# Routing one half of the heads per copy of a sample's rows, narrower projections, and S5's zeroth powers as copies, in a two-layer decoder step

## The chip, the cores and the metric

One core of a Trainium2 chip. The metric is the device time of one execution in microseconds (us), lower is better. Engines: PE (TensorE), DVE (VectorE), ACT (ScalarE), POOL (GpSimd) and SP (SyncE, which only issues DMAs). Each engine runs its own instructions in the order in which the program gives them.

## The reference

One inference step of a decoder with two layers. There are 512 prompt tokens and 64 sample tokens (8 sequences of 8), 576 in all, of width 1024.

- Layer 0 mixes tokens with S5, a grouped complex-diagonal state space (64 groups of 16 channels, 64 states each), then a GLU. Layer 1 mixes them with causal pooling over 2, 4, 8 or 16 tokens.
- After each mixer, and after each channel mixer, `x <- LN(ALPHA * x + f(x))`.
- The channel mixer of both layers is PEER: `q = x @ w_q` gives 8 heads of two halves of 128. Each of these 16 halves (chunks `c` below, head `c // 2`) is scored against 128 keys; the best 16 of each half are kept; of the 16 x 16 sums per head the best 16 are kept. These name 128 x 128 experts: `idx = i1 * 128 + i2`, `gate = softmax(best)`, `out = sum(gate * gelu(x . u[idx]) * v[idx])`.

```
s = einsum('thid,hind->thin', q, keys)
top_s, top_i = top_k(s, 16)
cand_s = top_s[:, :, 0, :, None] + top_s[:, :, 1, None, :]
best_s, best_j = top_k(cand_s, 16)
```

## The kernel before, in words

The tokens stand in five tiles of 128 rows. Tiles 0 to 3 are the prompt. Tile 4 holds the 64 sample tokens twice: rows 0 to 63 and rows 64 to 127 are copies. So 640 columns are projected (`NX`; `NT` is 576, `ND` is 384, the columns of tiles 0 to 2). Products are made from a high and a low part of each operand (`xH`, `xL` and `wh`, `wl`), three matmuls for one; `wl` is a subtraction on DVE, or on POOL for the weights `w_q`.

**S5.** `params` makes the powers 0 to 8 of the state matrix (`PW`). While PE projects the input, eight weights `m` of 128 columns in two halves each, `back(q)` makes on DVE the tile `BL` (powers 7 down to 0 times `bb`, four buffers, two a call) and `turn(q)` transposes it on PE into `BT`; ACT copies it out. `udone(m)` writes the projection to DRAM (`du`); it is read back as `U8`, half of the groups after `m = 3` and the other half after `m = 7`, eight DMAs each. Then `taps` makes `CL` on DVE (powers 0 to 8 times `c`), `inputs` multiplies `BT` with `U8` into `HS`, `toeplitz` makes `KT`, and `steps` runs the recurrence on DVE. The last `swap` (a DMA from `HS` to `H`) lets PE make the outputs.

**Norm and projection.** `out_proj` calls `norms`: tile by tile a residual, the norm (`layer_norm`: lines 791 to 801, small steps on one column between two large ones), the transposes of the tile on PE, and the split into `xH` and `xL`. After tiles 3 and 4 `early(0, ND)` projects the first two chunks of `w_q` for tiles 0 to 2; these wait in `self.pre`.

**Routing.** `peer` first stores tiles 0 to 2 to DRAM (`XD`) and adds `xH` and `xL` back into `xT` on POOL (line 1049). Then comes a loop over the 16 chunks: PE projects chunk `c` (`projected`) and scores chunk `c - 1` (`scores`: five matmuls, copied by ACT into one of three buffers `sc`), and DVE takes the best 16 of chunk `c - 2` (`tops`: `top16` on five tiles, five instructions for each: `MAX8`, `FIND_INDEX8`, `MATCH_REPLACE8`, `MAX8`, `FIND_INDEX8`). Between them a generator, `routing`, is pulled at most six times for each chunk. It runs `stage2` (the sums, their best 16, the experts' numbers and the gates) for four heads at a time and five tiles (heads 0 and 1, then 2 and 3, each on 10 rows of 128 x 256), so both calls end at chunk 12. After the loop `stage2` runs for tiles 3 and 4 with heads 4 to 7 (8 rows), then for tiles 0 and 1, then 2. With the experts of tiles 3 and 4 known, POOL begins to gather their rows.

**What stands beside the routing.** After the loop PE works on up to 44 of the 128 blocks of `u` (`raw` matmuls), stored with `spill`. How many, and between which instructions the generator is pulled, is decided by a count of costs when the program is written, not by time. Then follow the `hots` (one-hot products), and the long loop over 128 blocks of `u` and `v`, bound by PE.

Of the kernel before, what the change touches and what calls it, by code (L numbers as in the profile page):

```python
# [39 lines left out]
BT, GB, HC, PW = 1, 32, 2.0, (1,)  # L40
GE, S3, S4 = 0.98, 100, 4
VL = (43, 44, 45)
ORDER = [a for a in range(128) if (a + 1) * NPO // 128 > a * NPO // 128]
ORDER += [a for a in range(128) if a not in ORDER]
OFF = [0, 16, 24, 29, 33, 36, 38, 40] + list(range(42, 50))
# [81 lines left out]
class K:  # L127
# [142 lines left out]
    def s5(self):  # L270
# [55 lines left out]
        def powered(jobs, a, b):  # L326

            def args(e, w):
                n, k = e.stop - e.start, len(range(9)[w])
                sh = [128, n, k, 16]  # L330
                pw = [PW[:, w, r, e].rearrange("p s e -> p e s")[:, :, :, None].to_broadcast(sh) for r in range(2)]
                return pw, [t[:, e, None, :].to_broadcast(sh) for t in (a, b)]
            todo = [(o, t) + args(e, w) for o, t, e, w in jobs]
            for o, t, pw, ab in todo:
                V.tensor_tensor(o, pw[0], ab[0], op=OP.mult)
            for o, t, pw, ab in todo:
                V.tensor_tensor(t, pw[1], ab[1], op=OP.mult)
            for o, t, pw, ab in todo:
                V.tensor_tensor(o, o, t, op=OP.subtract)

        def params():
# [14 lines left out]
                next(ex, None)  # L356
            for _ in ex:
                pass
            V.memset(PW[:, 0, 0, :], 1.0)
            V.memset(PW[:, 0, 1, :], 0.0)  # L360
            V.tensor_tensor(PW[:, 1, 0, :], mag, cs, op=OP.mult)
            V.tensor_tensor(PW[:, 1, 1, :], mag, sn, op=OP.mult)
            tmp = p2.tile([128, 4, 8, 16], F32, name="BL", bufs=4).rearrange("p a b c -> p a (b c)")[:, :, :64]
            for b in (1, 2, 4):
                sh = [128, b, 64]
                cmul(V, PW[:, b + 1:2 * b + 1, 0, :], PW[:, b + 1:2 * b + 1, 1, :],
# [3 lines left out]
            im = slice(64, 128)  # L370
            A.activation(b2[im], b2[im], AF.Copy, scale=-1.0)
            A.activation(c1[im], c1[im], AF.Copy, scale=-1.0)

            for h in range(2):
                rows, e = slice(64 * h, 64 * h + 64), slice(32 * h, 32 * h + 32)
# [18 lines left out]

            for h in range(2):
                e = slice(32 * h, 32 * h + 32)
                BL = p2.tile([128, 4, 8, 16], F32, name="BL", bufs=4)
                t = BL.rearrange("p e s j -> p (e s) j")
                V.tensor_tensor(bb[:, e], bc(fr[:, e]), b1[:, e], op=OP.mult)
                V.tensor_tensor(t, bc(fi[:, e]), b2[:, e], op=OP.mult)  # L400
                V.tensor_tensor(b1[:, e], bc(fi[:, e]), b1[:, e], op=OP.mult)
                V.tensor_tensor(b2[:, e], bc(fr[:, e]), b2[:, e], op=OP.mult)
                V.tensor_tensor(bb[:, e], bb[:, e], t, op=OP.subtract)
                V.tensor_tensor(b2[:, e], b2[:, e], b1[:, e], op=OP.add)

        def back(q):

            BL, tb = ([p.tile([128, 4, n, 16], F32, name=k, bufs=m)[:, :, :8] for _ in range(2)] for p, k, n, m in ((p2, "BL", 8, 4), (pc, "tb", 9, 2)))
            e = [slice(8 * q + 4 * i, 8 * q + 4 * i + 4) for i in range(2)]
            powered([(BL[i], tb[i], e[i], slice(7, None, -1)) for i in range(2)], bb, b2)  # L410
            return BL

        def turn(q, BL):
# [7 lines left out]
        def taps(q):  # L421

            for e0 in (8 * q, 32 + 8 * q):
                es = [slice(e0 + i, e0 + i + 4) for i in (0, 4)]
                powered([(CL[:, e], pc.tile([128, 4, 9, 16], F32, name="tb", bufs=2), e, slice(0, 9)) for e in es], c1, c2)


        params()
# [9 lines left out]
        def udone(m, o):  # L438
            uT = p2.tile([128, NT], F32, name="uT", bufs=2)
            for q in range(2):  # L440
                A.activation(uT[:, 288 * q:288 * q + 288], o[q][:, :288], AF.Copy)
            A.dma_start(du[128 * m:128 * m + 128, :], uT)
            if m % 4 == 3:
                g = slice(8 * (m - 3), 8 * m + 8)
                for s in range(8):
                    (G if m > 3 and s % 2 else S).dma_start(U8[16 * s:16 * s + 16, g, :], duv[s][:, g, :])

        first = self.W.next_raws(2)
        o = [[self.ps(), self.ps()] for _ in range(2)]
# [361 lines left out]
    def projected(self):  # L811

        if self.pre:
            w, o, a, b = self.pre.pop(0)
            c, d = (b, NX) if a == 0 else (0, a)
            outs = [(self.ps()[:, :d - c], slice(c, d))]
            self.proj(outs, w, self.xH, self.xL)
            outs.insert(0 if a == 0 else 1, (o[:, :b - a], slice(a, b)))
        else:
            outs = [(self.ps()[:, :b - a], slice(a, b)) for a, b in ((0, ND), (ND, NX))]  # L820
            self.proj(outs, self.W.next(), self.xH, self.xL)
        return outs

    def finish(self, res, ln, p, then, transposed):
# [37 lines left out]
                    for _ in tr[4]:  # L862
                        pass
        if transposed:
            self.early(ND, NX)
            for tt in range(3):
                for _ in tr[tt]:
                    pass
# [163 lines left out]
    def peer(self, layer):  # L1032
# [10 lines left out]
        SD = self.dram.tile([128, 128, ND], F32, name=f"SD{layer}")  # L1043
        XD = self.dram.tile([128, 3, D], F32, name=f"XD{layer}")
        p2 = self.pool(rt, "pr2")

        S.dma_start(XD, self.x012)
        xT = self.per.tile([128, KD, ND], F32, name="x012")
        G.tensor_tensor(xT, self.xH.main.bitcast(F32), self.xL.main.bitcast(F32), op=OP.add)
        pr = self.pool(rk, "pr")  # L1050

        it = pr.tile([128, 128], I32, name="it")
# [1 line left out]
        self.iota2 = p2.tile([128, 128, 2], F16, name="iota2")  # L1054
        A.activation(self.iota2, it[:, :, None].to_broadcast([128, 128, 2]), AF.Copy)

        tops_ = [[pr.tile([128, 2, 5, 4, 16] if q < 2 else [128, 5, 8, 16], dt, name=f"{n}{q}") for q in (0, 2)]
                 for n, dt in (("tv", F32), ("ti", U32))]
        tv, ti = (lambda tt, c, t=t: t[0][:, c // 4, tt, c % 4] if c < 8 else t[1][:, tt, c - 8] for t in tops_)
        LG = ExitStack()  # L1060
# [22 lines left out]
        kload(0)  # L1083
        kload(1)

        def scores(c, q):
            o = [self.psB(), self.psB()]
            sc = pq.tile([128, 5, 128], F32, name="sc", bufs=3)
            for tt in range(5):
                d = o[tt // 4][:, 128 * (tt % 4):128 * (tt % 4) + 128]  # L1090
                self.mm(d, q[:, 128 * tt:128 * tt + 128], keys[c // 4][:, c % 4, :], True, True)
            A.activation(sc[:, :4].rearrange("p a b -> p (a b)"), o[0], AF.Copy)
            A.activation(sc[:, 4], o[1][:, :128], AF.Copy)
            return sc

        def tops(c, sc):
            self.top16([(sc[:, tt], tv(tt, c), ti(tt, c)) for tt in range(5)])

        prev = prev2 = None
        for c in range(16):  # L1100
            outs = self.projected()
            self.W.ahead()
            if layer == 0:
                next(self.pt, None)
            if prev:
                s_ = (c - 1, scores(c - 1, prev))
                if c % 4 == 0 and c < 12:
                    kload(c // 4 + 1)
            q = pq.tile([128, NX], F32, name="q", bufs=2)
            for o, cols in outs:  # L1110
                A.activation(q[:, cols], o, AF.Copy)
            if prev2:
                tops(*prev2)
                self.scored = c - 2
                for _ in range(PA):
                    if self.half or next(bg) == STEP:
                        break
            prev2 = s_ if prev else None
            prev = q
# [237 lines left out]
    def routing(self, tops, p, pr, p2, rk, gidx, ggate, GD, kept, begin, ending):  # L1357
# [7 lines left out]
        for g in range(2):  # L1365
            while self.scored < 4 * g + 3:
                yield STEP
            yield from self.stage2(tv[0][:, g], ti[0][:, g], p2, [t[:, :, 32 * g:32 * g + 32] for t in out])
        self.half = 1
        yield 0.0  # L1370
        unit = lambda ts: self.stage2(tv[1][:, ts], ti[1][:, ts], p2, [t[:, ts, 64:] for t in out])
        i1, i2, gate = out
        yield from unit(slice(3, 5))
        for u in range(2):
            f = p2.tile([128, 128], F32, name="idf")
            V.scalar_tensor_tensor(f, i1[:, 3 + u], 128.0, i2[:, 3 + u], op0=OP.mult, op1=OP.add)
            if u == 0:
                V.tensor_copy(gidx[:, :128], f)
                V.tensor_copy(ggate[:, :128], gate[:, 3])
            else:  # L1380
                for q in range(2):
                    rows = slice(64 * q, 64 * q + 64)
                    V.tensor_copy(gidx[rows, 128:], f[rows, rows])
                    V.tensor_copy(ggate[rows, 128:], gate[rows, 4, rows])
        self.gready = True
        yield 1.6

# [68 lines left out]
    def stage2(self, tv, ti, p, out):  # L1456
# [3 lines left out]
        V, A = nc.vector, nc.scalar  # L1460
        nt, nh = tv.shape[1], tv.shape[2] // 2
        n8 = nt * nh
        T = lambda n, w, dt=F32: p.tile([128, 10, w], dt, name=n)[:, :n8]
        v = tv.rearrange("p t (h s) k -> p (t h) s k", s=2)
        ids = p.tile([128, 10, 2, 16], F16, name="ids")[:, :n8]
# [24 lines left out]
        rep, hot, prod = (p.tile([128, 10, 16, 16], F16, name=k)[:, :n8] for k in ("rep", "hot", "prod"))  # L1490
# [143 lines left out]
```

## Time and profile before

| | |
|---|---|
| runs | 3201.87, 3198.44, 3200.00 us; median 3200.0 |
| profiled execution | 3198.16 us, span of the core 3195.9 us |
| busy in the span | PE 2993.5 us (94%), DVE 2713.2 (85%), POOL 1270.6 (40%), ACT 1150.6 (36%) |
| granted TensorE clock, mean | 0.972 of 2.4 GHz |
| chain that ended last, by engine | PE 73%, DVE 18%, DMA 5%, issue 2%, ACT 1%, POOL 1% |

The span is what the core's records cover; the execution's own time is 2.26 us longer. The chain follows the last instruction back, at each step to what released it, so its shares say where an earlier end would shorten the whole.

### The profile page before, as it was taken

To read this page: it belongs to the slowest core of one execution; us is meant where nothing else is said; L and a number is where in the kernel's file an instruction comes from. 1 tells how busy PE (TensorE), PEld (TensorE's weight loads), DVE (VectorE), ACT (ScalarE), POOL (GpSimd) and SP (SyncE) were. 2 spreads that over 40 slices of the span, in tenths; PEclk is the share of its full clock that TensorE was granted. 3 is DMA by queue.
4 is the path that set the end of the run, shared out by engine and by line. 5 is a ranking of instruction groups with operands and counts; after the bars stand their busy time and mean duration, and the time that the engine had idled before them with its cause. 6 is when DMAs were issued, how large, how long until landed. Compare 5 with 4: busy or idle time off the path is not lost.

```text
span 3195.9 us, 45180 instructions
## 1 busy us (share of the span) xinstructions
PE 2993.5 (94%) x16188; PEld 2549.7 (80%) x16188; DVE 2713.2 (85%) x5872; ACT 1150.6 (36%) x1712; POOL 1270.6 (40%) x944
## 2 busy tenths in 40 slices
PE   9589989998999999999978997989899999999996
PEld 7488965666888888888878896556688888888886
DVE  8956998998888888888986689899888888888888
ACT  2451323454333333333324132245433333333332
POOL 2321214443455555555410131444344545554541
PEclk9899989999999999999999999999999999999998
DMA  5461428899999999999943121889899999999995
GB/s 164 75 204 64 182 68 297 324 370 319 324 348 332 338 342 340 336 339 347 346 167 97 66 73 55 284 312 385 304 332 330 338 337 342 340 332 351 352 335 200
DMA packets 330416, 862.42 MB, mean 270 GB/s; under 512 B 54152, under 2 KB 143272, under 8 KB 327479
## 3 DMA queue, kind: packets, MB, share of 16 engines
q1 hardware_dynamic: 202574, 433.80, 39.2%
q0 software_dynamic: 113216, 405.95, 35.1%
q10 hardware_dynamic: 14400, 19.78, 1.7%
q8 instruction: 127, 2.08, 0.3%
q14 instruction: 99, 0.80, 0.1%
HBM read 791.76 MB, written 71.96 MB: 270 GB/s over the span
## 4 chain that ended last, share of the span: by engine, by line
PE 73%; DVE 18%; DMA 5%; issue 2%; ACT 1%; POOL 1%; SPq 1%; DVEq 0%; POOLq 0%; ACTq 0%
PE pa L133 42%; PE pb L133 30%; DMA grow<-in_peer_u,gidx 1%; DVE prod L1502 1%; DVE ti L1355 1%; DVE sc L1351 1%; DVE ti L1349 1%; DVE grow L1541 1%; DMA x<-SD 1%; DVE tv L1347 1%; DVE tv L1353 1%; DVE rs L799 1%; POOL grow L1536 1%; DVE prod L1520 0%; DVE st L783 0%
## 5 line engine op out<-in xcount | busy, mean ns | idle before, releaser
L1536 POOL DMA_INDIRECT grow<-in_peer_u,gidx x384 | 608.4, 1584 | 533.2 <-DVE acc L1549 309.5
L1536 POOL DMA_INDIRECT grow<-in_peer_v,gidx x384 | 499.8, 1302 | 711.0 <-DVE grow L1541 576.8
L138 DVE TENSOR_TENSOR vl<-vr,vh 128x1024 fp32r<-128x1024 f32 x256 | 314.3, 1228 | 250.6 <-ACT vh L137 250.2
L133 PE MATMUL pa<-vh,wwh 128*128 128x512 f32 x1536 | 478.6, 393 | 25.6 <-ACT wwh L1233 25.4
L1549 DVE SCALAR_TENSOR_TENSOR acc<-grow,gact,acc 128x1024 f32<-128x1024 f32 x380 | 486.9, 1281 | 3.4 <-DMA grow<-in_peer_v,gidx 2.4
L1541 DVE SCALAR_TENSOR_TENSOR grow<-grow,x 128x1024 f32<-128x1024 f32 x384 | 466.3, 1220 | 23.4 <-DMA grow<-in_peer_u,gidx 23.3
L133 PE MATMUL pa<-vh,wwl 128*128 128x512 f32 x1536 | 477.3, 392 | 0.0
L133 PE MATMUL pa<-vl,wwh 128*128 128x512 f32 x1536 | 476.5, 392 | 0.0
L137 ACT ACTIVATE vh<-vr 128x1024 fp32r<-128x1024 f32 x256 | 271.8, 1062 | 509.9 <-PE pa L133 480.8
L133 PE MATMUL pb<-xH,wl 128*128 128x384 f32 x1344 | 455.1, 339 | 0.0
L133 PE MATMUL pb<-xH,wh 128*128 128x384 f32 x1344 | 455.0, 339 | 0.0
L133 PE MATMUL pb<-xL,wh 128*128 128x384 f32 x1344 | 454.5, 338 | 0.0
L133 PEld LDWEIGHTS pa<-vh,wwh 128*128 128x128 f32 x1536 | 287.1, 189 | 76.8 <-ACT wwh L1233 28.9
L133 PEld LDWEIGHTS pa<-vl,wwh 128*128 128x128 f32 x1536 | 289.4, 188 | 63.4
L133 PEld LDWEIGHTS pa<-vh,wwl 128*128 128x128 f32 x1536 | 288.6, 188 | 63.4 <-DVE wwl L1235 1.4
L133 PEld LDWEIGHTS pb<-xL,wh 128*128 128x128 f32 x1344 | 253.2, 188 | 7.4
L133 PEld LDWEIGHTS pb<-xH,wh 128*128 128x128 f32 x1344 | 252.4, 188 | 6.5
L133 PEld LDWEIGHTS pb<-xH,wl 128*128 128x128 f32 x1344 | 252.4, 188 | 0.0
L79 POOL TENSOR_TENSOR wl<-wr,wh 128x1024 fp32r<-128x1024 f32 x35 | 88.9, 2541 | 408.2 <-ACT wh L69 314.3
L79 DVE TENSOR_TENSOR wl<-wr,wh 128x1024 fp32r<-128x1024 f32 x185 | 225.5, 1219 | 23.7 <-ACT wh L69 23.6
L133 PE MATMUL pb<-x,wr 128*128 128x384 f32 x704 | 240.5, 496 | 0.1
L69 ACT ACTIVATE wh<-wr 128x1024 fp32r<-128x1024 f32 x220 | 230.9, 1050 | 11.3 <-PE pa L133 11.3
(341 smaller groups left out, 4853.5 us busy)
## 6 DMA issues: line engine op xcount, KB each, us to landing
wr<-in_U SPq DMA_DIRECT2D x256, 512.0 KB
vr<-in_peer_v SPq DMA_DIRECT2D x256, 512.0 KB
GD<-stg SPq DMA_DIRECT2D x16, 2048.0 KB
x<-GD SPq DMA_DIRECT2D x64, 512.0 KB
SD<-g ACTq DMA_DIRECT2D x88, 192.0 KB
x<-SD SPq DMA_DIRECT2D x88, 192.0 KB
wr<-in_w_q SPq DMA_DIRECT2D x32, 512.0 KB
grow<-in_peer_u,gidx POOLq DMA_INDIRECT x384, 7.4
```

Of the source, the lines that this page charges most:

```text
L69: self.k.nc.scalar.activation(h[:, :nk], self.raw[self.nh], AF.Copy)
L79: e.tensor_tensor(l[:, :nk], self.raw.pop(self.ns), h[:, :nk].bitcast(F32), op=OP.subtract)
L133: self.nc.tensor.matmul(out, lhsT, rhs, start=start, stop=stop)
L137: self.nc.scalar.activation(h, src, AF.Copy)
L138: self.nc.vector.tensor_tensor(l, src, h.bitcast(F32), op=OP.subtract)
L799: yield V.scalar_tensor_tensor(t, y, ve, y, op0=OP.mult, op1=OP.mult)
L1347: V.max(v[:, 0:8], s)
L1349: V.max_index(i[:, 0:8], v[:, 0:8], s)
L1351: V.match_replace(s, v[:, 0:8], s, -3.0e38)
L1536: nc.gpsimd.indirect_dma_start(out=t, out_offset=None, in_=table, in_offset=bass.IndirectOffsetOnAxis(ap=gidx[:, 128 * u + j:128 * u + j + ...
L1541: V.scalar_tensor_tensor(t, t, 1.0, self.X(3 + u), op0=OP.mult, op1=OP.mult, accum_out=act[:, 128 * u + j:128 * u + j + 1])
L1549: V.scalar_tensor_tensor(acc[:, u], t, w, acc[:, u], op0=OP.mult, op1=OP.add)
```

## The change

1. S5: power 0 is no longer computed. ACT copies `c1` into `CL[:, :, 0]` and `bb` into `BL[:, :, 7]`; the DVE products are 7 and 8 powers wide, not 8 and 9. `BL` has six buffers, not four. `U8` is read in four parts, after `m` = 3, 5, 6 and 7 (groups 0 to 31, 32 to 47, 48 to 55, 56 to 63), each as four DMAs on SP and four on POOL.
2. The projections of `w_q` and of the pooling mixer end at column 576: the second matmul of each pair has 192 columns, not 256.
3. Tile 4 after the scores: rows 0 to 63 hold the even heads of the samples, rows 64 to 127 the odd ones. `top16` runs on tile 4 once for two chunks (`c % 4 > 1`), and `stage2` in the loop has four tiles (8 rows), not five (10); tile 4 goes with tile 3 after the loop, as before 8 rows. The numbers and gates of tile 4 are taken with fewer and narrower copies.
4. The scores of chunks 0 and 1 for tiles 0 to 2, and their `top16`, are issued at the start of `peer`, from the early projections; the loop then makes only the rest of these two chunks.
5. The store of `XD` stands behind the loads of the keys, and `xT` is added in three parts, in chunks 1, 2 and 3 (3, 3 and 2 of 8 slices), not at once at the start.

```diff
+UL = {3: 0, 5: 4, 6: 6, 7: 7}
...
-            V.memset(PW[:, 0, 0, :], 1.0)
-            V.memset(PW[:, 0, 1, :], 0.0)
...
+            A.activation(CL[:, :, 0], c1, AF.Copy)
...
-            BL, tb = ([p.tile([128, 4, n, 16], F32, name=k, bufs=m)[:, :, :8] for _ in range(2)] for p, k, n, m in ((p2, "BL", 8, 4), (pc, "tb", 9, 2)))
+            BL, tb = ([p.tile([128, 4, 8, 16], F32, name=k, bufs=m) for _ in range(2)] for p, k, m in ((p2, "BL", 6), (pc, "tb", 2)))
...
-            powered([(BL[i], tb[i], e[i], slice(7, None, -1)) for i in range(2)], bb, b2)
+            for i in range(2):
+                A.activation(BL[i][:, :, 7], bb[:, e[i]], AF.Copy)
+            powered([(BL[i][:, :, :7], tb[i][:, :, :7], e[i], slice(7, 0, -1)) for i in range(2)], bb, b2)
...
-                powered([(CL[:, e], pc.tile([128, 4, 9, 16], F32, name="tb", bufs=2), e, slice(0, 9)) for e in es], c1, c2)
+                powered([(CL[:, e, 1:], pc.tile([128, 4, 8, 16], F32, name="tb", bufs=2), e, slice(1, 9)) for e in es], c1, c2)
...
-            if m % 4 == 3:
-                g = slice(8 * (m - 3), 8 * m + 8)
+            if m in UL:
+                g = slice(8 * UL[m], 8 * m + 8)
...
-                    (G if m > 3 and s % 2 else S).dma_start(U8[16 * s:16 * s + 16, g, :], duv[s][:, g, :])
+                    (G if s % 2 else S).dma_start(U8[16 * s:16 * s + 16, g, :], duv[s][:, g, :])
...
-            outs = [(self.ps()[:, :b - a], slice(a, b)) for a, b in ((0, ND), (ND, NX))]
+            outs = [(self.ps()[:, :b - a], slice(a, b)) for a, b in ((0, ND), (ND, NT))]
...
+        def begin_scores(c):
+
+            q, sc = pq.tile([128, NT], F32, name="q", bufs=2), pq.tile([128, 4, 128], F32, name="sc", bufs=3)
+            A.activation(q[:, :ND], self.pre[c][1][:, :ND], AF.Copy)
+            o = self.psB()
+            for tt in range(3):
+                self.mm(o[:, 128 * tt:128 * tt + 128], q[:, 128 * tt:128 * tt + 128], keys[0][:, c, :], True, True)
+            A.activation(sc[:, :3].rearrange("p a b -> p (a b)"), o[:, :ND], AF.Copy)
+            begun.append((q, sc))
+
...
+            self.mm(o[1][r, :128], q[:, SEQ:], k, True, True)
+            A.activation(sc[:, t0:].rearrange("p a b -> p (a b)"), o[0][:, 128 * t0:], AF.Copy)
+            if c % 4 < 2:
+                sc4[c % 4] = pq.tile([128, 128], F32, name="sc4", bufs=4)
+            A.activation(sc4[c % 2][r], o[1][r, :128], AF.Copy)
...
+            sets = [(sc[0][:, tt], tv(tt, c), ti(tt, c)) for tt in tiles or range(3 if c < 2 else 0, 4)]
+            if c % 4 > 1 and not tiles:
+                sets.append((sc[1],) + tuple(t[1][:, 4, 2 * (c // 4) + c % 2] for t in tops_))
...
+        for c in range(2):
+            begin_scores(c)
+        for c in range(2):
+            tops(c, (begun[c][1],), range(3))
...
+            if 0 < c < 4:
+                ks = slice(3 * c - 3, min(3 * c, KD))
+                G.tensor_tensor(xT[:, ks], *(t.main[:, ks].bitcast(F32) for t in (self.xH, self.xL)), op=OP.add)
...
-            yield from self.stage2(tv[0][:, g], ti[0][:, g], p2, [t[:, :, 32 * g:32 * g + 32] for t in out])
+            yield from self.stage2(tv[0][:, g], ti[0][:, g], p2, [t[:, :4, 32 * g:32 * g + 32] for t in out])
```

## Rows read from the trace of the kernel before

**Rows 1.** Windows: us, busy of PE, PEld, DVE, ACT, POOL, then clock, DMA.
```profile
306.90:339.60 32.70, 32.70 (x236) 32.70 (x236) 18.39 (x121) 9.42 (x20) 10.10 (x5) 0.96 0.42 156
339.60:455.60 116.00, 97.25 (x669) 95.69 (x668) 114.61 (x630) 38.31 (x66) 29.46 (x11) 0.93 0.31 114
...
540.00:577.00 37.00, 30.04 (x88) 17.56 (x88) 34.70 (x105) 8.91 (x19) 19.35 (x15) 0.86 0.88 303
```

**Rows 2.** Chain in order of time, layer 0's routing: start us, us, what.
```profile
331.17 6.89 PE pa L133 x48
...
339.62 1.06 DVE tv L1347 x5
...
466.71 0.95 DVE tv L1347 x5
...
472.87 0.91 DVE cand L1472 x7
```

**Rows 3.** The same chain in layer 1's routing.
```profile
1863.76 1.06 DVE tv L1347 x5
...
1996.66 0.91 DVE cand L1472 x7
```

**Rows 4.** Timeline of PE behind the loop, layer 0: [idle before <- releaser].
```profile
546.12 0.48 PE L1396 MATMUL pa<-ident,i 128*128 128x128 f32 x1 [6.25 <-DVE i L1504]
...
580.56 1.89 PE L133 MATMUL pa<-BA 128*128 128x128 f16 x16 [4.23 <-DVE BA L1419]
```

**Rows 5.** Timeline of DVE in the routing, layer 0.
```profile
315.60 1.07 DVE L1347 MAX8 tv<-sc 128x8 f32<-128x128 f32 x5 [8.17 <-ACT sc L1092]
...
362.83 3.46 DVE L1510 TENSOR_TENSOR prod<-hot,off 128x2560 f16<-128x2560 f16 x1
...
415.35 1.49 DVE L1510 TENSOR_TENSOR prod<-hot,off 128x2560 f16<-128x2560 f16 x1
...
472.58 0.29 DVE L1466 CAST ids<-ti 128x256 f16<-128x256 uint32 x1
...
482.24 1.22 DVE L1508 TENSOR_TENSOR hot<-rep,off 128x2048 f16<-128x2048 f16 x1 [1.56 <-ACT rep L1492]
...
495.00 0.39 DVE L1504 TENSOR_TENSOR i<-prod 128x128 f32<-128x128 f16 x1
```

**Rows 6.** Timelines of POOL and of DVE in the norm of tile 3.
```profile
288.22 6.82 POOL L1049 TENSOR_TENSOR x<-xH,xL 128x3072 f32<-128x3072 f32 x1 [1.62 <-DVE rs L800]
...
288.24 6.81 DVE L799 SCALAR_TENSOR_TENSOR rs<-rs 128x1 f32<-128x1 f32 x1
```

**Rows 7.** Timeline of PE, layer 1: 384 beside 256 columns; then 384 beside 192 (x2).
```profile
1700.27 0.34 PE L133 MATMUL pa<-xH,wl 128*128 128x384 f32 x1
...
1700.57 0.34 PE L133 MATMUL pa<-xH,wh 128*128 128x384 f32 x1
...
1731.23 0.45 PE L133 MATMUL pa<-pH,wh 128*128 128x384 f32 x2
1731.52 0.45 PE L133 MATMUL pa<-pL,wh 128*128 128x384 f32 x2
```

**Rows 8.** Timelines of DVE, PE and POOL in S5, and the chain behind it.
```profile
65.20 1.29 DVE L335 TENSOR_TENSOR BL<-PW,bb 128x512 f32<-128x512 f32 x2 [1.96 <-PE pb L417]
...
69.95 1.29 DVE L335 TENSOR_TENSOR BL<-PW,bb 128x512 f32<-128x512 f32 x2 [1.05 <-PE pb L417]
...
73.57 1.42 DVE L335 TENSOR_TENSOR CL<-PW,c 128x576 f32<-128x576 f32 x2
...
106.05 0.71 DVE L552 TENSOR_TENSOR w<-AP,HS 128x512 f32<-128x512 f32 x1
...
97.69 6.04 PE L133 MATMUL pa<-U,BT 128*64 128x72 f32 x128 [5.77 <-issue]
...
84.54 2.76 POOL L446 DMA_DIRECT2D U<-du  x4 [46.51 <-DMA du<-uT]
...
146.54 2.32 DMA H<-HS
```

More of the change, by code (lines that the diff above doesn't have):

```diff
@@ L358, in params @@
                 pass
-            V.memset(PW[:, 0, 0, :], 1.0)
-            V.memset(PW[:, 0, 1, :], 0.0)
             V.tensor_tensor(PW[:, 1, 0, :], mag, cs, op=OP.mult)
             V.tensor_tensor(PW[:, 1, 1, :], mag, sn, op=OP.mult)
-            tmp = p2.tile([128, 4, 8, 16], F32, name="BL", bufs=4).rearrange("p a b c -> p a (b c)")[:, :, :64]
+            tmp = p2.tile([128, 4, 8, 16], F32, name="BL", bufs=6).rearrange("p a b c -> p a (b c)")[:, :, :64]
             for b in (1, 2, 4):
@@ L396, in params @@
                 e = slice(32 * h, 32 * h + 32)
-                BL = p2.tile([128, 4, 8, 16], F32, name="BL", bufs=4)
+                BL = p2.tile([128, 4, 8, 16], F32, name="BL", bufs=6)
                 t = BL.rearrange("p e s j -> p (e s) j")
@@ L814, in projected @@
             w, o, a, b = self.pre.pop(0)
-            c, d = (b, NX) if a == 0 else (0, a)
+            c, d = (b, NT) if a == 0 else (0, a)
             outs = [(self.ps()[:, :d - c], slice(c, d))]
@@ L864, in finish @@
         if transposed:
-            self.early(ND, NX)
+            self.early(ND, NT)
             for tt in range(3):
@@ L1045, in peer @@
         p2 = self.pool(rt, "pr2")
-        S.dma_start(XD, self.x012)
-        xT = self.per.tile([128, KD, ND], F32, name="x012")
-        G.tensor_tensor(xT, self.xH.main.bitcast(F32), self.xL.main.bitcast(F32), op=OP.add)
         pr = self.pool(rk, "pr")
@@ L1055, in peer @@
         A.activation(self.iota2, it[:, :, None].to_broadcast([128, 128, 2]), AF.Copy)
-        tops_ = [[pr.tile([128, 2, 5, 4, 16] if q < 2 else [128, 5, 8, 16], dt, name=f"{n}{q}") for q in (0, 2)]
+        tops_ = [[pr.tile([128, 2, 4, 4, 16] if q < 2 else [128, 5, 8, 16], dt, name=f"{n}{q}") for q in (0, 2)]
                  for n, dt in (("tv", F32), ("ti", U32))]
@@ L1084, in peer @@
         kload(1)
+        S.dma_start(XD, self.x012)
+        xT = self.per.tile([128, KD, ND], F32, name="x012")
+        sc4, begun = {}, []
+        def begin_scores(c):
[6 more added lines that the diff above has]
+            begun.append((q, sc))
@@ L1086, in scores @@
         def scores(c, q):
             o = [self.psB(), self.psB()]
[L1088 to L1094, printed above, removed]
@@ L1096, in tops @@
-        def tops(c, sc):
-            self.top16([(sc[:, tt], tv(tt, c), ti(tt, c)) for tt in range(5)])
+            t0 = 3 if c < 2 else 0
+            sc = begun[c][1] if c < 2 else pq.tile([128, 4, 128], F32, name="sc", bufs=3)
+            k, r = keys[c // 4][:, c % 4, :], slice(c % 4 // 2 * 64, c % 4 // 2 * 64 + 64)
+            for tt in range(t0, 4):
+                self.mm(o[0][:, 128 * tt:128 * tt + 128], q[:, 128 * tt:128 * tt + 128], k, True, True)
+            self.mm(o[1][r, :128], q[:, SEQ:], k, True, True)
@@ new lines, in scores, with tops @@
+            A.activation(sc[:, t0:].rearrange("p a b -> p (a b)"), o[0][:, 128 * t0:], AF.Copy)
+            if c % 4 < 2:
+                sc4[c % 4] = pq.tile([128, 128], F32, name="sc4", bufs=4)
+            A.activation(sc4[c % 2][r], o[1][r, :128], AF.Copy)
+            return sc, sc4[c % 2]
+        def tops(c, sc, tiles=None):
+            sets = [(sc[0][:, tt], tv(tt, c), ti(tt, c)) for tt in tiles or range(3 if c < 2 else 0, 4)]
+            if c % 4 > 1 and not tiles:
+                sets.append((sc[1],) + tuple(t[1][:, 4, 2 * (c // 4) + c % 2] for t in tops_))
+            self.top16(sets)
@@ L1108, in peer @@
                     kload(c // 4 + 1)
-            q = pq.tile([128, NX], F32, name="q", bufs=2)
-            for o, cols in outs:
+            q = begun[c][0] if c < 2 else pq.tile([128, NT], F32, name="q", bufs=2)
+            for o, cols in outs[1 if c < 2 else 0:]:
                 A.activation(q[:, cols], o, AF.Copy)
@@ L1373, in routing @@
         yield from unit(slice(3, 5))
-        for u in range(2):
+        for u, c in ((0, slice(0, 128)), (1, slice(64, 128))):
             f = p2.tile([128, 128], F32, name="idf")
[L1376 to L1384, printed above, removed]
+            V.scalar_tensor_tensor(f[:, c], i1[:, 3 + u, c], 128.0, i2[:, 3 + u, c], op0=OP.mult, op1=OP.add)
+            o = slice(64 * u + c.start, 64 * u + c.stop)
+            V.tensor_copy(gidx[:, o], f[:, c])
+            V.tensor_copy(ggate[:, o], gate[:, 3 + u, c])
         self.gready = True
@@ L1462, in stage2 @@
         n8 = nt * nh
-        T = lambda n, w, dt=F32: p.tile([128, 10, w], dt, name=n)[:, :n8]
+        T = lambda n, w, dt=F32: p.tile([128, 8, w], dt, name=n)[:, :n8]
         v = tv.rearrange("p t (h s) k -> p (t h) s k", s=2)
-        ids = p.tile([128, 10, 2, 16], F16, name="ids")[:, :n8]
+        ids = p.tile([128, 8, 2, 16], F16, name="ids")[:, :n8]
         V.tensor_copy(ids, ti.rearrange("p t (h s) k -> p (t h) s k", s=2))
@@ L1489, in stage2 @@
         sh = [128, n8, 16, 16]
-        rep, hot, prod = (p.tile([128, 10, 16, 16], F16, name=k)[:, :n8] for k in ("rep", "hot", "prod"))
+        rep, hot, prod = (p.tile([128, 8, 16, 16], F16, name=k)[:, :n8] for k in ("rep", "hot", "prod"))
         yield STEP
```

## The prediction

> **What bounds the kernel now.** I read the chain by engine first, then the windows, then the chain in order of time, then single engines' timelines where the chain changes hands. PE holds most of the chain, but an edit to PE's work helps only where PE is what ends last, so the reader should look for the stretches where another engine does. There are two kinds that this change touches. In the routing of each layer the chain runs on PE until 339.62 and then stays on DVE, piece after piece, to the end of the loop over chunks at 472.87 [rows 2]; DVE is busy 114.61 of 116 us there while PE has 18.75 us idle [rows 1]. Before that point it is the reverse: PE is busy all of 32.7 us and DVE only 18.39 [rows 1], for DVE waits for scores (8.17 us before the first maxima) [rows 5]. Behind the loop PE still meets DVE late: it waits 6.25 us for the experts' numbers and 4.23 us for the one-hot products [rows 4]. So from 339.62 to 580.56 every us that DVE sheds is one that the end sheds, and layer 1 repeats it (133.25 us from the first maxima on the chain to the next stage's sums in layer 0, 132.9 in layer 1) [rows 2, 3]. In S5 the chain is DVE's as well, from its last `BL` to the recurrence's last step, and then a DMA [rows 8]. Everything in the long loops over 128 blocks is untouched and bound by PE; it only moves.
>
> **Maxima and sums (parts 3 and 4).** Five sets of maxima take 472.58 - 466.71 = 5.87 us [rows 2, 5], so one set is 1.17. Before, each chunk has five sets. After, chunks with c % 4 of 0 or 1 have four, those with 2 or 3 have five. Of the chunks whose maxima lie in the DVE-bound stretch (3 to 15) six lose a set (4, 5, 8, 9, 12, 13): 6 x 1.17 = 7.0 us a layer. The sets of chunks 0 to 2 that go or move to the front save nothing: they stood where DVE idles, and the next maxima wait for PE's scores anyway. That is why I give the early maxima of tiles 0 to 2 no price of their own.
>
> `stage2` with 8 rows is shown: from 472.58 to 495.39, less 1.56 of waiting for ACT, is 21.25 us [rows 5]. With 10 rows it stands between the maxima. The stretch from 339.62 to 472.58 is 132.96 us; 13 chunks of 5.87 leave 56.65 for two calls, 28.3 each, with some DVE instructions that POOL held up in it (the product of 2560 took 3.46 us once and 1.49 the other time) [rows 5]. By proportion it would be at most 21.25 x 10 / 8 = 26.6. The saving of a call lies between nothing (all fixed cost) and 7.05 (28.3 - 21.25); I take 4.4, since the instructions' own parts fall from 1.49 to near 1.22 for 2560 against 2048 and little of a call is fixed. Two calls: 8.8 us. The narrower copies of tile 4's numbers save some 0.4 more. Together 16.2 us a layer.
>
> Does PE follow? Its own work is 97.25 us in the 116 us stretch, so it has 18.75 us to give up before it becomes the bound there [rows 1], and the 10.5 us of waits behind it [rows 4] take up a difference. The pulls of the generator stay in the same chunks: a call loses one step of its 21, both calls still end at chunk 12, and what remains behind the loop has the same costs, so the number of `u` blocks worked off beside it stays.
>
> **The move of xT, and the early scores (parts 4 and 5).** At 288.24 a DVE instruction on one column takes 6.81 us and ends with POOL's add of `xT`, which began at 288.22 and took 6.82 [rows 6]. One holds up the other, in the middle of the norm. The Trainium skill, page "SBUF — State Buffer", section "Who interferes with whom", says that a DVE instruction with two SBUF inputs waits for a whole GpSimd instruction that reads SBUF; the trace agrees with its 6.81 us. After, the add goes to chunks 1 to 3 as 2.6, 2.6 and 1.7 us (3, 3 and 2 eighths of 6.82), where DVE has 14.3 us idle [rows 1] and PE needs POOL once a chunk for a 2.7 us subtraction (29.46 us for 11 [rows 1]); it costs nothing there. Without that idle time it would cost its 6.8 us again. What the norm gains is between 0 and 6.6 us a layer. Against it stands that PE now has to go through both early scores, each behind an ACT copy and ahead of another, before the rest of chunk 0: four copies of about 0.47 us (9.42 us for 20 [rows 1]) and six small matmuls between them, which I put at 3.5 us. PE also has the early projections to finish before tile 4's transposes, so not all of 6.6 arrives. Net bounds -1 to 3; I take 0.5 a layer.
>
> **Narrower projections (part 2).** Nothing in w_q is shown with 192 columns, but a pair of 384 and 192 is, in the pooling mixer: 1731.52 - 1731.23 = 0.29 us. The pair of 384 and 256 takes 6.89 / 24 = 0.287 us in w_q [rows 2] and 0.30 in the pooling mixer [rows 7]. So w_q gains nothing, and pooling at most 8 chunks x 24 pairs x 0.013 = 2.5 us; DVE's windows lie close behind there, so I take 1.3 (0 to 2.5). The Trainium skill speaks for more: page "TensorE: Matmul & The Clock Gate", section "Back-to-back issue gap", gives N / 2.4 + 2.5 ns a matmul, by which 64 columns fewer save 26.7 ns; the sum would be some 9 us larger by it. The same page's "LDWEIGHTS" section gives P / 1.2, 107 ns for 128 columns of weights, which would hide it, as the pair of 0.29 does.
>
> **S5 (part 1).** A call of `back` takes 73.57 - 69.95 = 3.62 us, six products of 0.603 on 512 elements. `taps` and two small adds fill 73.57 to 106.05; with 0.2 for each add, 48 products of 0.668 on 576 elements [rows 8]. 64 elements are 0.065 us. The last `back` waits for the transposes of two calls before it (until 65.20 the last but one, until 69.95 the last [rows 8]). With six buffers it waits for three calls before, so it starts at 65.2 and, at 0.538 a product, ends at 68.4. Then 48 products of 0.603 and 0.4 put the first step at 97.8 in place of 106.05, 8.3 us earlier. It needs the second half of `HS`, for which PE waited 5.77 us until 97.69, some 13 us after the last `U8` issues began (84.54) [rows 8]. A last part of a quarter of the groups should need about a quarter of that, so PE can start when it is free, at 91.9, and end at about 98. I take 7.8 us for what reaches the DMA at 146.54 [rows 8] and all that hangs on it. The 17 small ACT copies are not in the trace; ACT is not on this chain, and they cost nothing unless DVE is made to wait for them (below). Bounds: -2.7 to 8.3.
>
> **Sum.** 2 x (16.2 + 0.5) + 1.3 + 7.8 = 42.5 us. From the profiled execution, 3198.16, that gives 3155.7; the median of the runs shown lies 1.8 us higher, so I say 3156 us.
>
> **Rivals.**
> - Narrow matmuls do pay by the column. A pair of 640 columns takes 0.287 us [rows 2], 0.45 ns a column, so 64 fewer in 24 pairs would be 0.69 us a chunk; some 4 PE-bound chunks in each layer and 8 pooling chunks make 11.0 us, 9.7 more than the 1.3 in the sum: 3146. The pair of 0.29 with 192 columns speaks against it [rows 7]. Chance 0.10. It is what the Trainium skill's issue-gap rule named above would do.
> - The routing's saving arrives by half. The stretch behind the loop also has POOL's first gathers in it, whose DMAs load the same queues as PE's weights (DMA share 0.88 from 540 to 577 [rows 1]); if these hold the end, 16.7 of 33.4 us go, and the time is 3172. For it: PE is 7 us idle in 37 there, not more. Against it: both waits in [rows 4] are for DVE. Chance 0.16.
> - S5 turns a wait into another. If DVE's products have to wait for ACT's copy into the same `BL`, that copy stands on ACT behind the transposes of the call before: with 4.75 us a call, the last `back` starts at about 76 and the first step at 108.7, 2.7 us late. Total 32 us, 3166. Nothing in the rows decides it. Chance 0.10.
> - It gets slower: POOL's subtractions and the parts of `xT` fall beside DVE's two-input instructions and hold them up by some 2 us each (3.46 against 1.49 [rows 5]). It takes 22 more such meetings to eat 42.5 us; POOL has 11 subtractions in the stretch of a layer [rows 1] and three parts of `xT`, so nearly all would have to meet. Time above 3200. Chance 0.03.
> - The change is made but the loop is held by something that DVE hid, and nothing is left but scatter: 0.03.
>
> **How the numbers follow.** The forecast itself has 0.58 and its own terms spread from 3147 to 3164. The range 3140 to 3177 takes in the first three rivals and leaves out the last two and the tails. A measurement of this kernel tells 0.2%, 6.4 us, from no change; all but the last two cases lie beyond that: faster 0.94, same 0.03, slower 0.03.
>
> **What would show it.** The first step of S5's recurrence at about 98 us, and PE's outputs 8 us earlier; no long one-column instruction in the norms; DVE-bound stretch of the routing some 16 us shorter in both layers, PE's idle time in it cut by as much; pairs of 384 and 192 columns still at 0.287 us; as many stored blocks of `u` as before. It is wrong if the stretch behind the loop grows by what the loop lost, if the last `BL` starts after 70, or if projections run faster than 0.287 a pair.

## The result, and the profile after

| | before | after |
|---|---|---|
| median of 4 runs, us | 3199.22 (3195.78 to 3201.87) | 3164.01 (3160.56 to 3170.63) |
| ratio, 95% interval | | 0.9893 (0.9872 to 0.9914) |
| profiled execution and span, us | 3198.16, 3195.9 | 3161.16, 3159.4 |

The forecast was 3156 us, 3140 to 3177. The page of the changed kernel, busy times and the chain's shares by engine:

```profile
PE 2996.0 (95%) x16188; PEld 2544.2 (81%) x16188; DVE 2661.5 (84%) x5674; ACT 1153.0 (36%) x1733; POOL 1274.0 (40%) x960
...
PE 75%; DVE 15%; DMA 5%; ACT 2%; issue 2%; SPq 1%; POOL 0%; DVEq 0%; ACTq 0%; POOLq 0%
```

DVE lost 51.7 us of work, PE none; what the time lost is a part of DVE's share of the chain. The timelines of S5, which answer to [rows 8]:

```profile
65.23 1.16 DVE L337 TENSOR_TENSOR BL<-PW,bb 128x448 f32<-128x448 f32 x2 [1.45 <-PE pb L420]
...
97.75 0.68 DVE L555 TENSOR_TENSOR w<-AP,HS 128x512 f32<-128x512 f32 x1
...
91.06 0.29 PE L135 MATMUL pa<-U,BT 128*64 128x72 f32 x2
...
91.19 4.25 PE L135 MATMUL pa<-U,BT 128*64 128x72 f32 x126
...
140.79 4.49 PE L135 MATMUL pa<-H,CL 128*64 128x72 f32 x62 [17.81 <-DMA H<-HS]
```

The last product into `BL` stands 4.72 us earlier, the first step 8.30 and PE's outputs 8.26 (149.05 before). The routing of layer 0 on DVE, which answers to [rows 5, 6]:

```profile
276.36 1.99 DVE L802 SCALAR_TENSOR_TENSOR rs<-rs 128x1 f32<-128x1 f32 x1
...
279.97 0.22 DVE L802 SCALAR_TENSOR_TENSOR rs<-rs 128x1 f32<-128x1 f32 x1
...
298.21 0.68 DVE L1375 MAX8 tv<-sc 128x8 f32<-128x128 f32 x3 [1.46 <-ACT sc L1097]
...
321.79 1.06 DVE L1375 MAX8 tv<-sc 128x8 f32<-128x128 f32 x5 [6.85 <-ACT sc L1108]
...
330.13 1.07 DVE L1375 MAX8 tv<-sc 128x8 f32<-128x128 f32 x5 [2.40 <-ACT sc L1108]
...
449.52 0.98 DVE L1495 TENSOR_TENSOR cand<-tv 128x128 f32<-128x128 f32 x7
```

The 6.81 us on one column are gone. From 330.13, the maxima of chunk 3, DVE waits for next to nothing (0.7 us, for ACT) until the `cand` behind the loop; before, the same two points are 339.62 and 472.87. The windows of these two stretches (columns as in [rows 1]), changed kernel first, kernel before second:

```profile
330.13:449.61 119.48, 111.19 (x708) 102.39 (x707) 117.48 (x668) 40.23 (x71) 27.14 (x11) 0.97 0.34 119
```
```profile
339.62:472.87 133.25, 114.50 (x723) 106.05 (x722) 131.84 (x748) 41.81 (x72) 29.46 (x11) 0.94 0.32 112
```

DVE still fills the stretch, 13.8 us shorter, and PE's idle time in it fell from 18.8 to 8.3; PE's own work in it fell by 3.3. But the chain no longer goes over to DVE where the stretch begins. It stays on PE for another 16 us, passes through ACT's queue, and reaches DVE at 349.42, with the first one-hot product of `stage2`, for which DVE has waited 0.66 us (0.60 in layer 1):

```profile
346.18 0.40 ACT sc L1108
...
347.52 1.80 ACT rep L1515
...
349.42 1.24 DVE hot L1531
```

What DVE sheds between 330.13 and that point would no longer reach the end; with a faster PE (`equal_halves`, below) the wait is gone. The windows of DVE's work on the maxima alone (us, DVE, clock, DMA), up to the end of the loop's last maxima, changed kernel first:

```profile
330.13:449.31 119.18, 69.80 (x472) 0.97 0.34 119
```
```profile
339.62:472.58 132.96, 76.80 (x520) 0.94 0.32 112
```

Behind the loop PE meets DVE late at the same two instructions as before [rows 4], 4.02 and 3.35 us in place of 6.25 and 4.23:

```profile
525.14 0.33 PE L1419 MATMUL pa<-ident,i 128*128 128x128 f32 x1 [4.02 <-DVE i L1527]
...
558.92 1.09 PE L135 MATMUL pa<-BA 128*128 128x128 f16 x16 [3.35 <-DVE BA L1442]
```

Stage by stage, each from one timeline row to the next (PE's first output of S5, the transposes of tile 3, the first `cand` behind the loop, PE's first product of the long loop, DVE's first addition into `x` behind it, and the same in layer 1). The third column is the changed kernel's second trace (`after_again`, below); the last is the range over the ten other traces below.

| stage, us | before | after | again | others |
|---|---|---|---|---|
| S5, to PE's outputs | 149.1 | 140.8 | 140.2 | |
| to the transposes of tile 3 | 132.1 | 132.0 | 131.5 | 130.7 to 133.4 |
| routing, layer 0 | 191.7 | 176.7 | 176.7 | |
| behind its loop | 284.6 | 283.7 | 283.5 | 279.9 to 290.0 |
| long loop, layer 0 | 883.9 | 887.1 | 885.2 | 884.4 to 888.1 |
| to tile 3's transposes, layer 1 | 162.7 | 161.4 | 160.0 | |
| routing, layer 1 | 192.5 | 176.4 | 176.4 | |
| behind its loop | 286.6 | 287.1 | 282.1 | 282.6 to 290.0 |
| long loop, layer 1, to the end | 912.7 | 914.1 | 911.1 | 910.9 to 916.2 |

### The profile page after: what moved, and what is told of

The parts are those of the page before. It is cut to its first block, busy times and chain, and to the rows that moved or that the text cites. A ratio compares the mean times of both kernels' runs of the same rounds, so it can differ in the third digit from the quotient of the medians.

```text
span 3159.4 us, 45061 instructions
## 1 busy us (share of the span) xinstructions
PE 2996.0 (95%) x16188; PEld 2544.2 (81%) x16188; DVE 2661.5 (84%) x5674; ACT 1153.0 (36%) x1733; POOL 1274.0 (40%) x960
## 4 chain that ended last, share of the span: by engine, by line
PE 75%; DVE 15%; DMA 5%; ACT 2%; issue 2%; SPq 1%; POOL 0%; DVEq 0%; ACTq 0%; POOLq 0%
PE pa L135 44%; PE pb L135 30%; DMA grow<-in_peer_u,gidx 2%; DVE prod L1525 1%; DMA x<-SD 1%; DVE grow L1564 1%; DVE ti L1383 1%; DVE sc L1379 1%; DVE ti L1377 1%; DVE tv L1381 1%; DVE tv L1375 1%; DVE prod L1547 0%; ACT stg L1471 0%; DVE hot L1531 0%; DMA wr<-in_U 0%
```

## Experiments

Each is the changed kernel with the edit shown, unless it says otherwise. The ratio is to the kernel before, measured beside it, with its interval; for the changed kernel it is 0.9893 (0.9872 to 0.9914) and 0.9883 (0.9867 to 0.9900). Intervals of this width are 5 to 7 us to either side, so stages decide.

**Part 1 alone** (`s5_only`): the kernel before with the S5 lines of the diff.

> The kernel before with part 1 of the change alone (S5). By the prediction's steps the last product into BL starts at 65.2 us, the first step of the recurrence at 97.8 and PE's outputs near 141 instead of 149.05; everything behind only moves, so the time is about 8.3 us below the kernel before (3191). The rival says that the S5 stage's gain meets a wait further on, for the GLU's and the output's weights: then the output projection begins near 241.8 as before and the time is that of before.

Measured 0.9976 (0.9965 to 0.9987). PE's outputs came at 139.47 in an execution whose last transposes of S5 were 1.47 us early (77.36 against 78.83), so 8.1 us sooner; the output projection at 232.99 against 241.82, and the span is 3188.0 against 3195.9, 7.9 us less. The rival falls: nothing behind takes it back.

**U8 in two halves again** (`two_loads`)

```diff
-            if m in UL:
-                g = slice(8 * UL[m], 8 * m + 8)
+            if m % 4 == 3:
+                g = slice(8 * (m - 3), 8 * m + 8)
...
-                    (G if s % 2 else S).dma_start(U8[16 * s:16 * s + 16, g, :], duv[s][:, g, :])
+                    (G if m > 3 and s % 2 else S).dma_start(U8[16 * s:16 * s + 16, g, :], duv[s][:, g, :])
```

> The changed kernel with U8 read in two halves, as before (after m = 3 on SP, after m = 7 on SP and POOL). DVE is still done with CL near 97.5, but PE gets the second half some 13 us after its issues, near 97, in place of 91.06: the first step starts between 102 and 105 instead of 97.75, and the time is 5 to 7 us above the changed kernel. If the landing did not depend on the size of the last part, nothing changes.

Timelines of PE and DVE:

```profile
99.56 5.54 PE L135 MATMUL pa<-U,BT 128*64 128x72 f32 x128 [7.51 <-issue]
...
105.56 0.69 DVE L555 TENSOR_TENSOR w<-AP,HS 128x512 f32<-128x512 f32 x1 [7.14 <-ACT HS L506]
```

DVE had been ready and waited 7.14 us; PE's outputs came at 148.5, 7.1 us behind the changed kernel's when the later start of this execution (0.60) is taken off. The ratio is 0.9907 (0.9890 to 0.9923). Without the smaller last load the rest of part 1 is worth 1 us.

**Four buffers again** (`four_buffers`): `bufs=6` of `BL` back to 4, in three places.

> The changed kernel with four BL buffers, as before. If the buffers are what lets the last call of back start at 65.23, it waits for the transposes of two calls before again, until 69.95; the first step of the recurrence starts at 102.3 and the time is 4.5 us above the changed kernel. If the narrower products alone made the gain, the first step stays within 1 us of 97.75.

The last call of `back` began at 68.46, the first step at 100.99, PE's outputs at 144.03. This execution was 1.52 us early by PE's last transposes (77.27 against 78.79); with that, the buffers are worth 4.76 us of the 8.3. Ratio 0.9900 (0.9884 to 0.9917).

**Five sets again** (`five_sets`)

```diff
+        more = tuple(pq.tile([128, 16], dt, name=n) for n, dt in (("mv", F32), ("mi", U32)))
...
+            if c % 4 < 2 and not tiles:
+                sets.append((sc[0][:, 3],) + more)
```

> The changed kernel, and in the chunks with c % 4 of 0 or 1 one more set of maxima on scores already used, into a place that nobody reads: the work of five sets a chunk is back. If what DVE sheds between the first maxima that hold it and the end of the loop reaches the end in full, six of the eight sets of a layer cost 1.09 us each, 6.5 us a layer, and the time is 13 us above the changed kernel. If only half arrives, because the gathers' and weights' DMAs hold the stretch behind the loop, it is 6.5 us. In both the loop's own end is 6.5 us later.

The stretch from the maxima of chunk 3 to `cand` took 125.7 us in both layers, 6.3 and 6.6 more; the routing stages 184.6 and 183.0 us. The ratio is 0.9942 (0.9925 to 0.9959), clear of the changed kernel's, 16 to 19 us above it; by the stages it is 14.6 us in both layers, of which some 1.6 belong to the entry of layer 0, where the clock fell (last section). A set costs 1.17 us, not the 1.09 that was expected: with DVE's work on the maxima 7.0 us shorter in the changed kernel (69.80 against 76.80), six sets are 7.0 us a layer. That half of it would be lost falls.

**Ten rows again** (`ten_rows`): `stage2`'s tiles for 10 rows, `tv` and `ti` with a fifth tile that holds zeros, `[t[:, :, 32 * g:32 * g + 32] for t in out]`.

> The changed kernel with stage2 in the loop on ten rows again, the two more rows with no use. The prediction's term was 4.4 us a call, 17.6 us for the four calls of both layers; the changed kernel's rows say 3.6 a call, 14.4 us in all. If only half arrives behind the loop it is 7 us.

The routing stages took 184.9 us in both layers, 8.2 and 8.5 more, 4.1 and 4.2 a call of `stage2`. Ratio 0.9927 (0.9910 to 0.9943), 11 to 14 us above the changed kernel.

**xT at the start again** (`xt_at_start`): the store of `XD` and the whole add as first lines of `peer`, as before.

> The changed kernel with the add of xT and the store of XD at the start of the routing again, one add of 6.8 us. A one-column DVE instruction of some 6.8 us is back in the norm of tile 3. If the end of the norms sets PE's last transposes alone, these come up to 6 us later, 12 us for both layers; if DVE's two waits in the norm of tile 4 (2.03 and 1.74 us) take up most of it, PE waits 2 to 3 us more a layer and the time is 4 to 6 us above the changed kernel.

The routing stages took 182.7 and 182.4 us, 6.0 more in each layer, and the ratio is 0.9911 (0.9894 to 0.9927). Timelines of POOL, DVE and PE in layer 0, and windows of 4 us (the figure before the last two is the granted clock):

```profile
277.71 6.82 POOL L1051 TENSOR_TENSOR x<-xH,xL 128x3072 f32<-128x3072 f32 x1 [1.62 <-DVE rs L803]
...
277.73 6.82 DVE L802 SCALAR_TENSOR_TENSOR rs<-rs 128x1 f32<-128x1 f32 x1
...
294.33 1.06 PE L911 MATMUL pb<-ident,x 128*128 128x128 f32 x8 [2.22 <-DVE x L804]
296.82 1.65 PE L135 MATMUL pb<-keys,q 128*128 128x128 f32 x6 [1.42 <-ACT q L1094]
299.50 1.65 PE L135 MATMUL pb<-keys,q 128*128 128x128 f32 x6 [1.02 <-ACT q L1094]
```
```profile
294.00:298.00 4.00, 2.24 (x13) 2.04 (x14) 1.48 (x3) 1.77 (x4) 0.00 (x0) 0.68 0.00 0
298.00:302.00 4.00, 2.98 (x15) 2.68 (x13) 2.91 (x20) 1.35 (x3) 0.00 (x0) 0.50 0.02 6
302.00:306.00 4.00, 4.00 (x22) 4.00 (x21) 4.00 (x29) 0.04 (x2) 0.00 (x0) 0.54 0.01 2
```

The lock of [rows 6], POOL's add holding up DVE's instruction on one column, is back to the hundredth. PE waits 2.2 us longer for it, as expected, but that wait comes ahead of the two for the early scores, and the clock falls from 2.4 to 1.2 GHz: six score matmuls take 1.65 us against 0.94, and the 48 behind them 7.57 against 5.34, where the changed kernel has 1.00 throughout. This is the other 3.7 us. The first theory had the size, but not this way to it.

**Early scores out** (`late_scores`, and once more `late_again`): `begin_scores` and the maxima from it are gone; chunks 0 and 1 go through the loop like the others.

> The changed kernel without the early scores and maxima of chunks 0 and 1 (part 4); the maxima of tile 4 are still taken once for two chunks. If the early maxima are worth nothing of their own, since DVE idles beside these chunks anyway, PE saves the 1.42 and 1.02 us that it waits for the early copies, the maxima of chunk 3 begin 2.4 us earlier in each layer, and the time is up to 5 us below the changed kernel. If DVE lacks the time that the early maxima gave it, the maxima of chunk 3 begin later than 330.13, by up to 7 us a layer.

> The kernel without early scores once more, with more rounds. Its first trace had the stretch from the transposes of tile 3 to the end of the loop over chunks 1.8 us shorter in each layer than the changed kernel. If that stands, it is 3 to 4 us below the changed kernel of the same call, about 0.1%; if the early scores were worth their waits, it is level or above.

The routing stages are 174.9 and 174.6 us in the first trace, 174.9 and 174.5 in the second: 1.8 us shorter than with the early scores, four times. The ratios are 0.9879 (0.9862 to 0.9895) and 0.9859 (0.9843 to 0.9876), lower than the changed kernel's (0.9893 and 0.9883) by 0.0014 and 0.0024, with overlapping intervals. The two traces have 577 us in the stages behind the loops, the most of all thirteen traces (566 to 574 in the others), so their spans (3161.0 and 3154.2) do not show the gain. That the early scores cost time in the routing is shown. That the kernel without them is faster as a whole is not: what it gains in the routing may be lost behind the loops, and two traces do not tell that from scatter.

**640 columns again** (`wide`): `NX` for `NT` in `projected`, `early` and `q`.

> The changed kernel with 640 columns in w_q and the pooling mixer's projection again, all else as changed. If a pair of matmuls is held by its two weight loads, a pair of 384 and 256 columns takes 0.287 us against 0.294 for 384 and 192, and PE's chunks in the routing get 0.18 us shorter; pooling loses at most 2 us: the time is within 2 us of the changed kernel. If columns were what is paid, it would be 11 us above.

Ratio 0.9893 (0.9876 to 0.9909), that of the changed kernel. But the chunks did not get shorter: the chain of layer 0 has 7.10 us, 7.08 and 7.38 for 48 matmuls, against 7.05 to 7.07, the routing stages are 1.1 and 2.6 us longer (in layer 1 the clock fell beside the early scores), and the stage with the pooling mixer 162.8 us, as in the kernel before. The expectation's 0.294 us a pair is a chunk's 7.07 us by 24, and these include the chunk's entry behind the scores. Inside a chunk a pair of 384 and 192 takes 0.287 us in the changed kernel, and one of 384 and 256 takes 0.287 in the kernel before. In `wide` it is 0.287 too, but 0.300 in every second chunk; that is open.

**Equal halves** (`equal_halves`)

```diff
+            outs = [... for a, b in ((0, 288), (96, ND)) if equal] or [... for a, b in ((0, ND), (ND, NT))]
```

> The changed kernel, where each chunk of w_q from 2 on is projected as two matmuls of 288 columns in place of 384 and 192. It leaves out columns: the second half projects columns 96 to 383 again in place of 288 to 575, so queries from column 288 on are not the reference's and other experts come out; the amount of work is the same. If each matmul pays for its own columns unless these are fewer than its weight load covers, a pair of 288 takes 0.267 us, as in the GLU (6.40 us for 24 pairs), against 0.294, the 24 pairs of a chunk 6.4 against 7.07, and the maxima of chunk 3 begin 2 us earlier in each layer. If a pair pays two weight loads whatever its columns are, it stays at 0.29.

Chains of layer 0, the changed kernel first:

```profile
321.49 7.07 PE pa L135 x48
328.55 1.27 PE pb L135 x10
```
```profile
321.12 6.57 PE pa L135 x48
327.69 1.25 PE pb L135 x10
```

Inside a chunk 576 columns in halves take 0.266 us a pair (the expectation had 0.267), 0.020 less than as 384 and 192. The maxima of chunk 3 did not come earlier, since here the clock fell beside the early scores (1.25 and 6.66 us in place of 0.94 and 5.34). The ratio is 0.9875 (0.9858 to 0.9891).

**The changed kernel once more** (`after_again`)

> The changed kernel once more, unchanged, beside the next one. By its own trace and those of its variants, the loops over 128 blocks take between 884 and 888 us in layer 0 whatever stands ahead of them; if the 3.1 us more of the first trace (887.06 against 883.95) is scatter, this trace may show anything between, and the ratio to the kernel before is 0.987 to 0.990. If the change itself lengthens that loop, it shows 887 again.

Its span is 3146.8 us, 12.6 below the first trace, and 10.6 of these lie in the five stages that the change leaves alone, 1.9 of them in the long loop of layer 0 (885.2); the stages that the change touches are 42.7 us below the kernel before. The long loop of layer 0 begins with PE at the low clock after a wait of 7.9 to 8.8 us for its first weights, and how soon the clock is back differs from trace to trace (after, then before, in a window that begins 11.1 us behind PE's last product ahead of that wait):

```profile
735.73:739.73 4.00, 4.00 (x14) 3.17 (x13) 3.08 (x7) 0.52 (x1) 1.66 (x2) 0.70 0.74 229
```
```profile
760.05:764.05 4.00, 4.00 (x18) 3.27 (x17) 2.91 (x5) 1.36 (x2) 1.83 (x2) 0.97 0.83 250
```

That is worth 0.9 us: the seventh pair of products begins 4.20 us behind the loop's first in the kernel before and 5.12 in the changed one. In the second trace it is 5.21, and yet this loop is 1.9 us shorter than the first trace's; so the start does not make the difference, and where the rest scatters is open.

## Why the prediction was right, and where its terms were off

The forecast case came, 8 us above its figure and inside its range. In the trace the stages that the change touches became 40.7 us shorter (42.5 forecast); the five others became 4.2 longer, which makes 36.5. In the second trace the five are 6.4 shorter than before, and over all kernels they sum to between 2493 and 2512 us. So the 4.2 us are scatter, not something given back. The forecast has a slip: 3155.7 and 1.8 are 3157.5, not 3156.

- **S5:** 8.3 against 7.8. Each point came as worked out: last `BL` 65.23 (65.2), PE's inputs 91.06 (91.9), first step 97.75 (97.8). The rival in which DVE waits for ACT's copy falls: what it waits for is still PE's transposes (1.45 us).
- **Maxima:** as forecast. DVE's work on the maxima in the stretch fell by 7.0 us in each layer (76.80 to 69.80, and 76.77 to 69.80), and a set is 1.17 us.
- **stage2:** the size was right, but not all of it arrived. In the loop a call handles two heads of five tiles, ten rows, not four heads. Less the 7.0 us of maxima, the stretches fell by 6.8 and 6.7 us for both calls, where the sum has 8.8. DVE's own work in the calls fell by 8.6 and 9.0 us, 4.3 to 4.5 a call (4.4). Given back were 1.1 and 1.6 us beside POOL and 0.7 and 0.6 in the wait for ACT. Meetings with POOL went on, at other places: the product of L1547 took 3.29 us at 366.55, against 1.22 at 468.86, where before it was those of L1510 and L1520. What DVE instructions take in the stretch of layer 0 beyond the shortest of their kind, each time beside a running subtraction of POOL, is 5.64 us before and 6.76 after. Timelines of DVE and POOL:

```profile
366.55 3.29 DVE L1547 TENSOR_TENSOR prod<-hot,ids 128x2048 f16<-128x2048 f16 x1
...
365.52 3.24 POOL L81 TENSOR_TENSOR wl<-wr,wh 128x1024 fp32r<-128x1024 f32 x1 [3.51 <-ACT wh L71]
```

- **Entry:** too small: 1.2 and 2.5 us (what the routing stages gained, 15.0 and 16.2, less the DVE stretches' 13.8 and 13.7), against 0.5. The lock itself was read rightly: POOL's 6.82 us are DVE's 6.82. As the Trainium skill, page "SBUF — State Buffer", section "Who interferes with whom", has it, a two-input DVE instruction waits for the whole GpSimd instruction; `xt_at_start` agrees. What the sum left out is the clock: in the kernel before it stood at 0.66 behind PE's 2.22 us wait, in the window from 305 to 309 us, and with the early scores behind the lock the loss is 6 us a layer. Without the lock, and without the early scores' 1.8, the entry gains 3.0 and 4.3 us (by `late_scores`).
- **Early scores:** priced at nothing for the maxima, which holds, and at 3.5 us for PE. On the chain, from the copies behind tile 4's transposes to the end of chunk 0's projection, they cost 3.2 us (294.83 to 304.88, against 294.46 to 301.33 in `late_scores`); 1.3 come back, since chunks 0 and 1 then have fewer scores left, and 1.8 us a layer stay in the routing stages.
- **Narrow projections:** w_q gained nothing, as said: inside a chunk a pair stays at 0.287 us. A chunk still became 0.33 us longer, by part 3 and not by part 2 (last section), a term that the sum has at nothing; the three full chunks on PE's part of the chain make 1.0 us a layer of it, an estimate from the two periods. The stage with the pooling mixer gained 1.3 and 2.7 us (1.3), and `wide` gives that back. The rival that narrow matmuls pay by the column falls as it was put.
- **Half the routing's saving lost** falls by `five_sets` and `ten_rows`. **Slower by meetings of POOL and DVE** falls by the result; the meetings cost 1.1 to 1.6 us a layer more. The rival in which something hidden holds the loop falls too, save that PE holds the first 16 us of the stretch.

The other signs came as well: 88 blocks of `u` are stored, as before. That the total is so near is in part luck: the terms that were too small (the entry by 0.7 and 2.0 us, S5 by 0.5) make up for most of what stage2 lost on the way.

## What to carry to other kernels

Find the stretch in which one engine waits for nothing and count only the work taken out of that; the same work beside its idle time was worth nothing or, put on the other engine's path, less than nothing. A new short wait is to be looked at together with the waits that stand next to it: of those at the start of the routing, two of 1.42 and 1.0 us cost only themselves in 11 of 16 layers and the clock too in 5, while one of 2.2 us, with them or without, left a granted clock of 0.50 to 0.71 in windows of 4 us, in 6 of 6. And where a kernel has stages that scatter by 5 us, compare stages, not spans.

## What was not expected of the hardware

**Narrow beside wide.** From one matmul's start to the next, a matmul of 192 columns takes 0.09 us, but the one of 384 behind it 0.20, against 0.17 behind one of 256 in the kernel before. Timeline of PE, changed kernel:

```profile
322.28 0.25 PE L135 MATMUL pa<-xHt,wl 128*128 128x192 f32 x1
322.37 0.36 PE L135 MATMUL pa<-xH,wh 128*128 128x384 f32 x1
322.56 0.25 PE L135 MATMUL pa<-xHt,wh 128*128 128x192 f32 x1
322.65 0.36 PE L135 MATMUL pa<-xL,wh 128*128 128x384 f32 x1
```

What the narrow one saves the next one pays; two of 288 save part of it. The Trainium skill, page "TensorE: Matmul & The Clock Gate", has both halves of it: by the rule in "Back-to-back issue gap" 192 columns are 82.5 ns (an estimate), which the trace's 0.09 bears out, and by "LDWEIGHTS" the load of 128 columns of weights is 107 ns, longer than that matmul. The first of these sections adds that its rule is for a single matmul by itself, and that in a stream of pairs of load and matmul both set the spacing; the prediction quotes the rule without this. The rows of the weight loads (PEld) show the load sticking out:

```profile
322.28 0.19 PEld L135 LDWEIGHTS pa<-xH,wh 128*128 128x128 f32 x1
322.39 0.19 PEld L135 LDWEIGHTS pa<-xHt,wh 128*128 128x128 f32 x1
322.57 0.19 PEld L135 LDWEIGHTS pa<-xL,wh 128*128 128x128 f32 x1
```

A row lasts 0.19 us, but the load at 322.39 begins 0.11 behind the one before it, which agrees with the 107 ns, and 0.02 behind the start of the narrow matmul at 322.37; in the kernel before, and with equal halves, each load begins with a matmul. Where 48 matmuls of 192 columns follow each other, at the start of the loop, they take 5.34 us, 0.111 each.

**A half-wide matmul among the scores.** By part 3 two of the ten score matmuls of a chunk, those of tile 4, have weights 64 columns wide and not 128. The ten then hold the chain for 1.27 us (above), where they held it for 1.11:

```profile
330.05 1.11 PE pb L133 x10
```

Timelines of PE from the last two of the ten on, changed kernel first, kernel before second:

```profile
321.05 0.43 PE L135 MATMUL pb<-keys,q 128*64 128x128 f32 x2
321.41 0.44 PE L135 MATMUL pa<-xH,wh 128*128 128x384 f32 x1
321.69 0.25 PE L135 MATMUL pa<-xHt,wh 128*128 128x192 f32 x1
```
```profile
322.77 0.39 PE L133 MATMUL pb<-keys,q 128*128 128x128 f32 x2
322.92 0.42 PE L133 MATMUL pa<-xH,wh 128*128 128x384 f32 x1
323.17 0.28 PE L133 MATMUL pa<-xHt,wh 128*128 128x256 f32 x1
```

From the first of these two to the second matmul of the projection it is 0.64 us against 0.40. The weight loads tell where it goes: among the scores they begin 0.11 us apart, but the first half-wide load begins 0.31 us behind the load ahead of it, and so does the first full one behind the pair. With both ends a full chunk comes every 8.34 us, not 8.01, though its pairs are as fast. All kernels with the half-wide matmuls have it (`late_scores`, `wide` and `equal_halves` too), the kernel before and `s5_only` do not; no run changes it alone.

**The clock beside the early scores.** Their two waits, 1.42 and 1.02 us, left the clock at full speed in both layers of both traces of the changed kernel. With the same two waits it fell in 5 of the 12 layers of the six variants that have them and no lock: layer 0 of `five_sets`, `four_buffers` and `equal_halves`, layer 1 of `wide` and `equal_halves`. Windows of `four_buffers`:

```profile
300.00:304.00 4.00, 2.78 (x15) 2.59 (x15) 2.54 (x17) 1.12 (x4) 0.00 (x0) 0.69 0.03 8
304.00:308.00 4.00, 4.00 (x20) 4.00 (x20) 4.00 (x27) 0.39 (x1) 0.00 (x0) 0.50 0.00 0
```

Its next maxima, of tile 3 in chunk 0, came 2.9 us late by it (10.19 us behind the first ones, against 7.26). What decides it no run here shows.
